# One layer of a Griffin decoder on one core: gates by Silu behind the chain's square root, and a written-out order for ScalarE and VectorE from the output projection's second group on

## The chip, the cores and the metric

The kernel runs on one core of a Trainium2 chip. The metric is the device time of one execution in microseconds. Of the kernel before, three runs were timed: median 1433.09 us (1432.62 to 1435.61).

## The reference

One token mixer of the kind "Griffin" and one gate from a per-layer embedding, for 1024 tokens of width 2048, in fp32 (names of the reference shortened):

```python
u = rms_norm(h, norm_pre) @ w_in              # 2048 -> 4096: gate half and x half
xc = causal_conv4(x_half) + conv_b
r, i = sigmoid(xc @ w_r + b_r), sigmoid(xc @ w_i + b_i)   # 8 blocks of 256
a = exp(-8 * softplus(lam) * r)
s = scan(s * a + sqrt(1 - a**2) * i * xc)     # along the tokens
y = (s * silu(gate)) @ w_out
h = h + rms_norm(y, norm_post)
out = h + sigmoid(h @ w_gate) * (p @ w_proj)  # the PLE block
```

## The kernel before

**Tiles and products.** Tokens lie along the free axis in two halves `h` of T = 512, channels on 128 partitions. The three large products (called x for `w_in`, y for `w_out`, h for `w_gate`) are taken by a Strassen-like scheme of seven products m1, m2, m7, m6, m3, m4, m5 of half the size. Each output tile `p` of each of the seven is a *unit*: 8 operand tiles times three matmuls of 128x128 by 128x512 (`mm3`, L116 to L118: high times high, high times low, low times high part), since every fp32 number is split in two parts of the matmul's type: `split` has ScalarE make the high part (L106) and VectorE the low one (L107). `m7` takes operands named t3, `m6` those named t2, `m4` t4, `m5` t1.

**The order of the work.** The program is a list of units. Each has stages some units ahead of its matmuls (`product`): LOAD (a DMA on SP's queue, 4 or 7 units ahead), ADD (the second block of the weight is accumulated onto it by a DMA that POOL issues, 5 ahead, L423), PART (the split, 3 ahead). `later` and `put` move stores to DRAM one or more units behind the tile that they store; POOL issues them too (L195). SP's and POOL's order is that of the program. ScalarE's, VectorE's and TensorE's is chosen by a scheduler. The main loop does this for each unit:

```python
            for f in late.pop(at, ()):
                f()
            for rank, j, f in sorted(begun.pop(at, ()), key=lambda b: b[:2]):
                f()
            s["mm"]()
```

**Stages.** The first half of the tokens goes through the x product, then the second; between the last products of x stand the block weights' matmuls (`ri`) and the chain steps. A *chain* step (h, n), n from 0 to 7, follows its `ri` unit for two channel tiles: on ScalarE two Sigmoids each for r and i (L310, L311), Tanh (L314), Exp (L318), three Squares (L319 to L321), Sqrt (L323); on VectorE the products and the scan in between and, for h = 1, the multiply by the gate (L335). It works in one buffer `rq`, so a chain step's first Sigmoid waits for the last multiply of the step before. The convolution of the next step and its split `x` (for the next `ri` unit) come behind the root. "Chain 1", "chain 3" below are the steps (1, 1) and (1, 3).

**Gates.** In `x_mm`, m4 of tile p gives gate g0_p of the first half, m5 that of the second (`gs`). Both are made by a Sigmoid into the PSUM bank (L582, L594) and a multiply on VectorE (L583, L595); g0_p is then multiplied by the recurrence's stored result (L584) and stored on POOL's queue.

**Behind the x product** come y's m1, m2, then in groups of four p the units m7, m6, m3, then m4; then the PLE block (`mm_ple`, four units of 48 matmuls, evacuations of tokens' half 0 on ScalarE, L694, of half 1 on VectorE, L696; each of the 32 tiles is stored); then y's m5; then h in the same manner, whose units end with `emit_out`. `norm_z1`, `norm_z2` make the post-norm's factors, `h_first` and `h_second` the sums of h, `fetch` reads stored operands back, `keep` splits them. Small tiles come from the pool `vecs` of seven buffers of 128x512; PSUM has eight banks.

## Time and profile before

| | |
|---|---|
| median of three runs | 1433.09 us |
| profiled execution | 1431.73 us, span 1430.0 us |
| mean granted TensorE clock | 0.986 |
| busy: TensorE, VectorE, ScalarE, GpSimd | 1384.3, 972.8, 719.3, 272.1 us |
| DMA | 358.81 MB, mean 251 GB/s |

Times in the profile count from the span's start. "Busy" counts instructions that do work; a wait is what an engine sat idle and the semaphore that ended it. A granted clock of 1.0 is 2.4 GHz, one of 0.5 is 1.2 GHz.

### The profile page before, as it was taken

Reading aid. Unit: us, or ns where it says so; the run is one execution under the profiler, and the core shown is the slowest. Engines: PE = TensorE matmul, PEld = TensorE weight load, DVE = VectorE, ACT = ScalarE, POOL = GpSimd, SP = SyncE. Lnnn points to the kernel's source line nnn. Section 1 sums busy time; section 2 is a strip of 40 time slices with the busy share of each in tenths; the row PEclk is TensorE's granted clock in tenths of the full one; section 3 lists DMA queues with packets and bytes.
Section 4 is the critical chain, followed back from the end, with each engine's and each line's share of the span. In section 5 each row is a group of like instructions: output and inputs, shape, how many; then the busy total and the mean of one; then the engine's idle time right before and its main releaser. Section 6 shows DMA issues by size and latency. Waiting matters only on the chain.

```text
span 1430.0 us, 17152 instructions
## 1 busy us (share of the span) xinstructions
PE 1384.3 (97%) x6025; PEld 1133.6 (79%) x6025; DVE 972.8 (68%) x1299; ACT 719.3 (50%) x936; POOL 272.1 (19%) x422
## 2 busy tenths in 40 slices
PE   9999999999999999989799999999999999999997
PEld 6888787878887888878677778888787887888886
DVE  8588768566665776777898954364479795538576
ACT  8332257475757543877888652332335334324332
POOL 0113331221211110111102421100242132211021
PEclk9999999999999999999999999999999999999999
DMA  9769899877767896576677999760899699989795
GB/s 356 249 229 311 279 304 249 251 166 215 186 178 179 273 313 203 157 216 206 191 261 262 340 334 263 175 205 35 290 354 365 219 357 351 268 214 290 235 331 177
DMA packets 125815, 358.81 MB, mean 251 GB/s; under 512 B 15904, under 2 KB 16288, under 8 KB 125728
## 3 DMA queue, kind: packets, MB, share of 16 engines
q1 hardware_dynamic: 83232, 210.88, 41.8%
q0 software_dynamic: 42496, 146.83, 39.6%
q8 instruction: 47, 0.77, 0.2%
q14 instruction: 40, 0.33, 0.1%
HBM read 277.95 MB, written 79.69 MB: 250 GB/s over the span
## 4 chain that ended last, share of the span: by engine, by line
PE 48%; issue 23%; DMA 11%; DVE 8%; ACT 5%; POOL 4%; SPq 0%; POOLq 0%; DVEq 0%; ACTq 0%
PE hm L118 5%; PE hm L117 5%; PE hm L116 5%; PE ym L116 5%; PE ym L118 5%; PE ym L117 5%; PE xm L118 3%; PE xm L117 3%; PE xm L116 3%; POOL sp L195 2%; DMA fxb<-sp 2%; POOL x_m L423 2%; DMA sp<-rq 1%; DVE xc L283 1%; PE pp L116 1%
## 5 line engine op out<-in xcount | busy, mean ns | idle before, releaser
L423 POOL DMA_DIRECT2D x_m<-in_w_in x64 | 57.8, 949 | 135.8 <-DVE wlo_x7m L107 17.8
L283 DVE SCALAR_TENSOR_TENSOR xc<-xbp,cst,xc 128x512 f32<-128x512 f32 x96 | 66.9, 746 | 0.4 <-ACT xc L280 0.3
L116 PE MATMUL ri<-x,whi_ri 128*128 128x512 f32 x128 | 50.0, 419 | 15.2 <-ACT x L106 15.2
L195 POOL DMA_DIRECT2D sp<-g x32 | 18.9, 633 | 210.6 <-DVE g L584 180.3
L117 PE MATMUL ri<-x,whi_ri 128*128 128x512 f32 x128 | 52.0, 407 | 0.5 <-DVE x L107 0.5
L118 PE MATMUL ri<-x,wlo_ri 128*128 128x512 f32 x128 | 51.4, 402 | 0.0
L717 POOL DMA_DIRECT2D out_t<-sg x32 | 17.5, 546 | 144.8 <-DVE sg L716 141.8
L423 POOL DMA_DIRECT2D h_m<-in_w_gate x32 | 28.7, 1031 | 83.0 <-DVE wlo_h4m L107 24.8
L116 PEld LDWEIGHTS ri<-x,whi_ri 128*128 128x128 f32 x128 | 25.0, 199 | 22.7 <-ACT x L106 17.1
L423 POOL DMA_DIRECT2D y_m<-in_w_out x32 | 29.1, 999 | 72.5 <-DVE wlo_y4m L107 26.9
L310 ACT ACT_TABLE_LOAD x12 | 15.4, 1283 | 38.6 <-DMA sp<-rq 21.3
L713 DVE TENSOR_TENSOR sg<-uh,hm 128x512 f32<-128x512 f32 x24 | 15.8, 685 | 25.3 <-PE hm L118 25.3
L280 ACT ACTIVATE xc<-xbp,cst 128x512 f32<-128x512 f32 x32 | 24.3, 805 | 14.8 <-DMA xbp<-sp 10.5
L106 ACT ACTIVATE x<-xc 128x1024 fp32r<-128x1024 f32 x16 | 16.8, 1053 | 28.8 <-DVE xc L283 28.8
L117 PEld LDWEIGHTS ri<-x,whi_ri 128*128 128x128 f32 x128 | 25.0, 196 | 7.6 <-DVE x L107 1.4
L195 POOL DMA_DIRECT2D sp<-ux x16 | 8.8, 551 | 113.4 <-DVE ux L577 104.8
L118 PEld LDWEIGHTS ri<-x,wlo_ri 128*128 128x128 f32 x128 | 24.9, 194 | 6.0
L310 ACT ACTIVATE rq<-ri,cst 128x512 f32<-128x512 f32 x32 | 21.2, 686 | 13.0 <-DVE g L335 6.9
L116 PE MATMUL pp<-p,whi_ple 128*128 128x512 f32 x64 | 25.7, 405 | 1.8 <-ACT p L106 1.8
L106 ACT ACTIVATE x_t<-xu 128x512 fp32r<-128x512 f32 x8 | 5.1, 634 | 44.0 <-DVE xu L349 43.9
L195 POOL DMA_DIRECT2D sp<-z x16 | 8.7, 546 | 91.4 <-DVE z L613 74.1
L107 DVE TENSOR_TENSOR x_t<-fxt,x_t 128x512 fp32r<-128x512 f32 x24 | 16.0, 690 | 14.6 <-ACT x_t L106 14.5
(722 smaller groups left out, 4956.7 us busy)
## 6 DMA issues: line engine op xcount, KB each, us to landing
x_m<-in_w_in SPq DMA_DIRECT2D x72, 512.0 KB, 5.6
x_m<-in_w_in POOLq DMA_DIRECT2D x64, 512.0 KB, 8.0
y_m<-in_w_out SPq DMA_DIRECT2D x40, 512.0 KB, 6.7
h_m<-in_w_gate SPq DMA_DIRECT2D x40, 512.0 KB, 8.8
y_m<-in_w_out POOLq DMA_DIRECT2D x32, 512.0 KB, 9.5
o<-sp SPq DMA_DIRECT2D x64, 256.0 KB, 6.6
h_m<-in_w_gate POOLq DMA_DIRECT2D x32, 512.0 KB, 9.2
raw_ri<-in_w_ri SPq DMA_DIRECT2D x16, 512.0 KB, 5.0
```

Of the source, the lines that this page charges most:

```text
L106: nc.scalar.activation(hi, src, AF.Copy)
L107: nc.vector.tensor_tensor(lo, src, hi.bitcast(F32), ALU.subtract)
L116: nc.tensor.matmul(ps, whi, ahi, start=start, stop=False, skip_group_check=more)
L117: nc.tensor.matmul(ps, whi, alo, start=False, stop=False, skip_group_check=more)
L118: nc.tensor.matmul(ps, wlo, ahi, start=False, stop=stop, skip_group_check=more)
L195: nc.gpsimd.dma_start(t, src)
L280: nc.scalar.activation(xc[:, s], xbp[:, s, 3 : T + 3], AF.Identity, bias=col(C_CB, ct), scale=col(C_CW + 48, ct))
L283: nc.vector.scalar_tensor_tensor(xc[:, s], xbp[:, s, j : j + T], col(C_CW + 16 * j, ct), xc[:, s], op0=ALU.mult, op1=ALU.add)
L310: nc.scalar.activation(R[:, s], banks[0][s], AF.Sigmoid, bias=col(C_BR, ct))
L423: nc.gpsimd.dma_start(u["raw"], w[(p, *ADDED[name])], accum_op=ALU.add)
L713: nc.vector.tensor_tensor(sg, part, b, ALU.subtract if h == 0 else ALU.add)
L717: later(1, lambda: nc.gpsimd.dma_start(out[h, :, dt, :], sg))
```

## The change

1. *Gates.* Sigmoid into PSUM and multiply become one Silu in place. From the second half's first `ri` unit on, gates are put in a list and issued on ScalarE behind the Sqrt of a chain step, two units after it in the program; those of m4 with p of 12 and more are issued at once.
2. *Main loop.* The stages PRE, LOAD and ADD now stand ahead of the late stores, PART behind them.
3. *By hand.* From the y product's second group on (`o2`, its first m7 unit) ScalarE and VectorE also follow the program. There PART comes behind the unit's evacuation; further evacuation work (`rest`) and splits of fetched operands (`next_turn`) behind that; fetched operands are used two units after their load is issued, not one.
4. *PLE.* The block moves behind y's m5, in eight units of 24 matmuls; all its evacuations are on ScalarE. The norm's factors are made in three steps; `h_first` begins in m5.

```diff
@@ main loop
             at = now[0]
+            todo = sorted(begun.pop(at, ()), key=lambda b: b[:2])
+            splits = [f for rank, j, f in todo if rank == PART]
+            for rank, j, f in todo:
+                if rank != PART:
+                    f()
             for f in late.pop(at, ()):
                 f()
-            for rank, j, f in sorted(begun.pop(at, ()), key=lambda b: b[:2]):
+            if not by_hand[0]:
+                for f in splits:
+                    f()
+            rest = s["mm"]()
+            if by_hand[0]:
+                for f in splits:
+                    f()
+            if rest:
+                rest()
+            now[0] += 1
+            for f in tail.pop(at, ()):
                 f()
-            s["mm"]()
-            now[0] += 1
@@ chain
-        nc.scalar.activation(Q, Q, AF.Sqrt)
+        root = nc.scalar.activation(Q, Q, AF.Sqrt)
+        if h == 1:
+            later(2, lambda: open_gates(root.ins))
@@ ahead of x_mm
+    def gate(f, at_once=False):
+        if waits_gates[0] and not at_once:
+            gates.append(f)
+        else:
+            f()
+
+    def open_gates(behind):
+        with tc.issue_after(behind):
+            for f in gates:
+                f()
+        gates.clear()
@@ x_mm, m4 and m5
-            nc.scalar.activation(b, g, AF.Sigmoid)
-            nc.vector.tensor_tensor(g, g, b, ALU.mult)
-            nc.vector.tensor_tensor(g, g, h0.pop(p), ALU.mult)
-            put((("b11", "b21")[s], n), yd, g)
+
+            def gated():
+                nc.scalar.activation(g, g, AF.Silu)
+                nc.vector.tensor_tensor(g, g, h0.pop(p), ALU.mult)
+                put((("b11", "b21")[s], n), yd, g)
+
+            gate(gated, p >= NK - 4)
...
-            nc.scalar.activation(b, g, AF.Sigmoid)
-            nc.vector.tensor_tensor(g, g, b, ALU.mult)
+            gate(lambda: nc.scalar.activation(g, g, AF.Silu))
@@ fetched operands (h_first, h_second and h_one likewise)
-            keep("h", name, n, t[:, 0])
+            next_turn(lambda: keep("h", name, n, t[:, 0]))
@@ mm_ple
-        for dd in range(4):
-            dt = 4 * i + dd
+        for dd in range(2):
+            dt = 2 * i + dd
...
-                if h == 0:
-                    nc.scalar.activation(t, b, AF.Copy)
-                else:
-                    nc.vector.tensor_copy(t, b)
+                nc.scalar.activation(t, b, AF.Copy)
@@ y product, PLE block
+    def begin_by_hand():
+
+        after.enter_context(tc.manual_schedule(engines={mybir.EngineType.Activation, mybir.EngineType.DVE}))
+        by_hand[0] = True
+
...
-    spread(o2 + 2, 0.75, fetches("y", yd, "b22"))
-    spread(o3 - 7, 1, fetches("y", yd, "t4"))
-    spread(o3, 1, fetches("y", yd, "t1"))
-    hook(len(orders) - 2, lambda: load_p(0))
-    hook(len(orders) - 1, lambda: load_p(1))
+    spread(o2 + 2, 0.75, fetches("y", yd, "b22"), 2)
+    spread(o3 - 7, 1, fetches("y", yd, "t4"), 2)
+    spread(o3, 1, fetches("y", yd, "t1"), 2)
+    hook(HAND, begin_by_hand)
     strassen("y", w_out, orders, emit_z, hooks, park=True, inserts=inserts_b)
...
-    for i in range(4):
-        plain(w_ple[i], f"ple{i}", lambda u, i=i: mm_ple(u, i))
...
+    for i in range(3):
+        hook(i, lambda i=i: norm_z(i, 0))
+    spread(1, 2, [lambda n=n: h_first(n) for n in range(3)], 2)
+    hook(4, lambda: load_p(0))
+    hook(5, lambda: load_p(1))
     strassen("y", w_out, [(p, "m5") for p in range(NB)], emit_z, hooks)
+    uses = {}
+    for i in range(KH):
+        plain(w_ple[i], f"ple{i}", lambda u, i=i: mm_ple(u, i), 512)
+        for f in uses.pop(i, ()):
+            do(f)
+        if i < 5:
+            got = []
+            do(lambda got=got, i=i: got.append(h_first(i + 3)))
+            uses.setdefault(i + 2, []).append(lambda got=got: got.pop()())
+        if i < 3:
+            do(lambda i=i: norm_z(i, 1))
```

**Where instructions move.** POOL, around the weight of x's m5, p = 12 (`x12_m5`), before:

```order
L195 DMA sp114_5145<-g0_11_5134 128x512
L423 DMA x11_m5_5050<-in_w_in 128x1024
L195 DMA sp115_5232<-g0_12_5221 128x512
L423 DMA x12_m5_5149<-in_w_in 128x1024
```

and in the change:

```order
L206 DMA sp113_5165<-g0_10_4962 128x512
L206 DMA sp114_5167<-g0_11_5108 128x512
L436 DMA x12_m5_5118<-in_w_in 128x1024
L206 DMA sp115_5211<-g0_12_5198 128x512
```

The accumulation onto `x12_m5` now stands ahead of the store of gate g0_12 and behind that of g0_11. (Numbers of spilled tiles `sp` count on and differ.)

ScalarE in chain 3, from its third Sigmoid to the split of `x12_m5`, before:

```order
L311 ACTIVATE rq1_3_5327<-ri1_3_10_5301,cst_80 128x512
L106 ACTIVATE whi_x14m4_5295<-x14_m4_5234 128x1024
L582 ACTIVATE xm4_12_5196<-g0_12_5221 128x512
L311 ACTIVATE rq1_3_5327<-ri1_3_11_5302,cst_80 128x512
L314 ACTIVATE rq1_3_5327<-rq1_3_5327,dk_90 128x512 x2
L318 ACT_TABLE_LOAD
L318 ACTIVATE rq1_3_5327<-rq1_3_5327,dk_90 128x512
L594 ACT_TABLE_LOAD
L594 ACTIVATE xm5_10_5241<-g5_5266 128x512
L318 ACT_TABLE_LOAD
L318 ACTIVATE rq1_3_5327<-rq1_3_5327,dk_90 128x512
L106 ACTIVATE whi_x12m5_5350<-x12_m5_5149 128x1024
```

and in the change, from the chain's start on (the split of `x12_m5` is the next row):

```order
L321 ACT_TABLE_LOAD
L321 ACTIVATE rq1_3_5301<-ri1_3_00_5273,cst_80 128x512
L321 ACTIVATE rq1_3_5301<-ri1_3_01_5274,cst_80 128x512
L612 ACT_TABLE_LOAD
L612 ACTIVATE g0_12_5198<-g0_12_5198 128x512
L106 ACTIVATE whi_x14m4_5269<-x14_m4_5208 128x1024
L322 ACT_TABLE_LOAD
L322 ACTIVATE rq1_3_5301<-ri1_3_10_5275,cst_80 128x512
L322 ACTIVATE rq1_3_5301<-ri1_3_11_5276,cst_80 128x512
L325 ACTIVATE rq1_3_5301<-rq1_3_5301,dk_90 128x512 x2
L329 ACT_TABLE_LOAD
L329 ACTIVATE rq1_3_5301<-rq1_3_5301,dk_90 128x512 x2
```

Gate `g5` (m5, p = 10) has left the place between the two Exps; gate g0_12 stands between the Sigmoids with a table load on each side, and the chain begins with a load.

ScalarE in the y product's m7 units, before:

```order
L106 ACTIVATE y_t22_6757<-fyt22_6714 128x512
L150 ACTIVATE sq_z0_60_6666<-z60_6664 128x512
L106 ACTIVATE y_t23_6760<-fyt22_6714 128x512
L106 ACTIVATE y_t24_6798<-fyt24_6763 128x512
L106 ACTIVATE y_t25_6801<-fyt24_6763 128x512
L106 ACTIVATE y_t26_6840<-fyt26_6804 128x512
L106 ACTIVATE y_t27_6843<-fyt26_6804 128x512
L106 ACTIVATE whi_y2m7_6678<-y2_m7_6479 128x1024
```

and in the change:

```order
L106 ACTIVATE y_t22_6725<-fyt22_6682 128x512
L153 ACTIVATE sq_z0_60_6634<-z60_6632 128x512
L106 ACTIVATE y_t23_6728<-fyt22_6682 128x512
L106 ACTIVATE whi_y2m7_6646<-y2_m7_6447 128x1024
L641 ACTIVATE z70_6674<-ym1_7_6510 128x512
L153 ACTIVATE sq_z0_70_6676<-z70_6674 128x512
L106 ACTIVATE whi_y3m7_6688<-y3_m7_6489 128x1024
L529 ACTIVATE uy0_6717<-ym7_0_6692 128x512
L529 ACTIVATE uy1_6762<-ym7_1_6737 128x512
L106 ACTIVATE whi_y0m6_6764<-y0_m7_6351 128x1024
L106 ACTIVATE y_t24_6768<-fyt24_6731 128x512
```

The splits of the weights for m7's third and fourth unit have moved ahead of the fetched operands y_t24 and those behind it, which m6 uses.

## Rows read from the trace of the kernel before

**Rows 1.** Page, part 1: busy us, share of the span, instructions, by engine.
```profile
PE 1384.3 (97%) x6025; PEld 1133.6 (79%) x6025; DVE 972.8 (68%) x1299; ACT 719.3 (50%) x936; POOL 272.1 (19%) x422
```

**Rows 2.** Waits of TensorE: engine, line, waited for, us in total, times, longest.
```profile
PE ri L116 <- ACT x L106: 15.2, 4, 7.6
PE ym L116 <- ACT whi_y2m L106: 3.5, 1, 3.5
PE ym L118 <- DVE wlo_y5m L107: 3.4, 2, 2.0
PE hm L116 <- ACT whi_h1m L106: 2.9, 1, 2.9
...
PE pp L116 <- ACT p L106: 1.8, 1, 1.8
```

**Rows 3.** Windows of core 0: length, busy us (instructions), clock, DMA share, GB/s.
```profile
678.80:705.80 27.00, 19.11 (x73) 14.88 (x73) 25.66 (x31) 20.83 (x27) 3.91 (x6) 0.87 0.55 154
616.80:640.30 23.50, 19.32 (x73) 15.32 (x72) 20.58 (x25) 16.01 (x21) 2.52 (x4) 0.85 0.62 188
839.00:857.00 18.00, 14.44 (x51) 10.93 (x50) 12.32 (x17) 11.88 (x20) 4.08 (x5) 0.81 1.06 352
1198.00:1215.00 17.00, 13.57 (x52) 10.42 (x51) 12.12 (x17) 11.07 (x17) 2.91 (x4) 0.90 1.04 355
```

**Rows 4.** Timeline of TensorE: start, us, engine, line, form, [idle before <-releaser].
```profile
626.55 0.79 PE L116 MATMUL ri<-x,whi_ri 128*128 128x512 f32 x1 [4.18 <-ACT x L106]
...
683.72 0.39 PE L117 MATMUL xm<-x_t,whi_x12m 128*128 128x512 f32 x1
...
684.63 0.39 PE L118 MATMUL xm<-x_t,wlo_x12m 128*128 128x512 f32 x1
692.63 0.79 PE L116 MATMUL ri<-x,whi_ri 128*128 128x512 f32 x1 [7.62 <-ACT x L106]
```

**Rows 5.** Timeline of ScalarE, chain 1, in front of the squares.
```profile
612.95 1.06 ACT L106 ACTIVATE whi_x8m<-x_m 128x1024 fp32r<-128x1024 f32 x1 [2.16 <-DMA x_m<-in_w_in]
```

**Rows 6.** Timeline of ScalarE, chain 3.
```profile
668.93 1.28 ACT L594 ACT_TABLE_LOAD   x1
...
670.85 1.28 ACT L318 ACT_TABLE_LOAD   x1
...
677.36 1.06 ACT L106 ACTIVATE whi_x12m<-x_m 128x1024 fp32r<-128x1024 f32 x1 [4.49 <-DMA x_m<-in_w_in]
```

**Rows 7.** Timeline of POOL there, and the landing of the accumulation (us, last).
```profile
667.82 0.56 POOL L195 DMA_DIRECT2D sp<-g  x1 [18.68 <-DVE g L584]
668.37 0.95 POOL L423 DMA_DIRECT2D x_m<-in_w_in  x1
...
x_m<-in_w_in POOLq DMA_DIRECT2D x1, 512.0 KB, 8.9
```

**Rows 8.** Timeline of ScalarE, y product's m7; landing of the weight's accumulation issued at 825.24.
```profile
845.48 0.63 ACT L106 ACTIVATE y_t<-fyt 128x512 fp32r<-128x512 f32 x1 [2.50 <-DMA fyt<-sp]
...
847.07 1.04 ACT L106 ACTIVATE whi_y2m<-y_m 128x1024 fp32r<-128x1024 f32 x1
...
y_m<-in_w_out POOLq DMA_DIRECT2D x1, 512.0 KB, 13.8
```

**Rows 9.** Timeline of ScalarE, h product's m7.
```profile
1198.37 0.63 ACT L106 ACTIVATE h_t<-fht 128x512 fp32r<-128x512 f32 x1 [7.33 <-DMA fht<-sp]
```

**Rows 10.** Groups by line: busy us, mean ns, idle before; ScalarE, then VectorE.
```profile
L582 ACT ACTIVATE xm<-g 128x512 f32<-128x512 f32 x16 | 9.5, 593 | 0.1
...
L583 DVE TENSOR_TENSOR g<-g,xm 128x512 f32<-128x512 f32 x16 | 10.9, 681 | 6.4 <-ACT xm L582 6.4
```

**Rows 11.** PLE block: a window, VectorE's wait for stores, landing of the stores.
```profile
1020.00:1035.00 15.00, 15.00 (x69) 12.44 (x68) 5.40 (x12) 4.25 (x7) 5.84 (x10) 0.95 1.04 368
...
DVE pp L696 <- DMA sp<-pp: 10.4, 4, 3.6
...
sp<-pp POOLq DMA_DIRECT2D x26, 256.0 KB, 7.0
```

More of the change, by code (lines that the diff above doesn't have):

```diff
@@ L127, in rstd_a, with rstd_n @@
         nc.scalar.activation(s, v, AF.Sqrt)
+        return v, s, r, t
+    def rstd_n(v, s, r, t):
         nc.vector.reciprocal(r, s)
@@ L155, in trunk_kernel @@
     st = {}
+    after = ExitStack()
     def unit(mm, stages):
@@ L180, in plain, with next_turn @@
         return u
-    late = {}
-    now, n_spills = [0], [0]
+    late, tail = {}, {}
+    now, n_spills, by_hand = [0], [0], [False]
+    def next_turn(f):
+        if by_hand[0]:
+            tail.setdefault(now[0], []).append(f)
+        else:
+            f()
     def later(k, f):
@@ L511, in mm @@
             elif name == "m2":
-                emit(p, 0, 0, b, None)
+                return emit(p, 0, 0, b, None)
             elif name == "m7":
@@ L522, in mm @@
             elif name == "m4":
-                emit(p, 1, 0, b, t[:, 1])
+                return emit(p, 1, 0, b, t[:, 1])
             elif name == "m5":
-                emit(p, 1, 1, b, t[:, 1])
-                emit(p, 0, 1, b, t[:, 0])
+                rests = emit(p, 1, 1, b, t[:, 1]), emit(p, 0, 1, b, t[:, 0])
+                return lambda: [f() for f in rests]
         products(key, w, orders, mm, pre, hooks, inserts)
+    gates, waits_gates = [], [False]
+    def gate(f, at_once=False):
+        if waits_gates[0] and not at_once:
+            gates.append(f)
+        else:
+            f()
[4 more added lines that the diff above has]
+        gates.clear()
     m1d, ud, xbank, h0 = {}, {}, {}, {}
@@ L616, in emit_z @@
         st["nz", h] = seen + 1
-        square(z, seen == 0, h, f"z{h}_{p}{i}")
+        return lambda: square(z, seen == 0, h, f"z{h}_{p}{i}")
     hd = {}
@@ L637, in use @@
             make_h(0, n, z, x)
-            keep("h", "b11", n, z[:, 0])
-            keep("h", "b21", n, z[:, 1])
+            next_turn(lambda: [keep("h", name, n, z[:, i]) for i, name in enumerate(("b11", "b21"))])
         return use
@@ L655, in use @@
             put(("t2", n), hold, x[:, 1])
-            keep("h", "t3", n, x[:, 0])
+            next_turn(lambda: keep("h", "t3", n, x[:, 0]))
         return use
@@ L713, in emit_out, with rest @@
             nc.vector.tensor_tensor(sg, part, b, ALU.subtract if h == 0 else ALU.add)
-            nc.scalar.activation(sg, sg, AF.Sigmoid, scale=-1.0 if (i, h) == (0, 1) else 1.0)
-        nc.vector.tensor_tensor(sg, sg, o[:, 0], ALU.mult)
-        nc.vector.tensor_tensor(sg, sg, o[:, 1], ALU.add)
-        later(1, lambda: nc.gpsimd.dma_start(out[h, :, dt, :], sg))
+        def rest():
+            if part is not None:
+                nc.scalar.activation(sg, sg, AF.Sigmoid, scale=-1.0 if (i, h) == (0, 1) else 1.0)
+            nc.vector.tensor_tensor(sg, sg, o[:, 0], ALU.mult)
+            nc.vector.tensor_tensor(sg, sg, o[:, 1], ALU.add)
+            later(1, lambda: nc.gpsimd.dma_start(out[h, :, dt, :], sg))
+        return rest
     def norm_x(h):
-        st["r1"] = rstd_a(st["acc", h], f"x{h}")
+        st["r1"] = rstd_n(*rstd_a(st["acc", h], f"x{h}"))
     def norm_x2(h):
@@ L729, in hook, with spread @@
         hooks.setdefault(at, []).append(f)
-    def spread(at, every, fs):
+    def spread(at, every, fs, lag=1):
         for i, f in enumerate(fs):
@@ L820, in trunk_kernel @@
             at(o + 6, lambda h=h, n=n: block_ri(h, n), True)
+            if h == 1 and n == 0:
+                at(o + 6, lambda n=n: waits_gates.__setitem__(0, True))
     at(o + 6, lambda: do(lambda: pools["swap"]()), True)
@@ L825, in trunk_kernel, with norm_z @@
     hooks = hooks_b
-    def norm_z1(h):
-        st["rz"] = rstd_a(st["acc", h], f"z{h}")
-    def norm_z2(h):
-        st["rstd2", h] = rstd_b(st["rz"], h, f"z{h}")
+    def norm_z(step, h):
+        if step == 0:
+            st["rz"] = rstd_a(st["acc", h], f"z{h}")
+        elif step == 1:
+            st["rz"] = rstd_n(*st["rz"])
+        else:
+            st["rstd2", h] = rstd_b(st["rz"], h, f"z{h}")
     orders, o2, o3 = grouped(range(NB), range(NB), [(p, "m4") for p in range(NB)])
+    HAND = o2
@@ L872, in trunk_kernel @@
+    spread(o2 - 1, 0.75, fetches("h", hold, "t2"), 2)
+    spread(o2 + 2, 0.75, [lambda n=n: fetch("h", {("b22", k): hd[1, 2 * k + 1] for k in (n, n + 1)}, "b22", n) for n in range(0, KH, 2)], 2)
+    spread(o3 - 8, 0.5, [lambda n=n: h_one("t4", n) for n in range(KH)], 2)
+    spread(o3 - 4, 0.5, [lambda n=n: h_one("t1", n) for n in range(KH)], 2)
     strassen("h", w_gate, orders, emit_out, hooks, early_out, True)
@@ L879, in trunk_kernel @@
             begun.setdefault(max(0, j - ahead), []).append((rank, j, f))
-    with ExitStack() as after:
+    with after:
         def opened(name):
```

29 lines of the change are left out of this document (6 added, 23 removed).

## The prediction

> **What bounds the kernel now.** The page's busy line comes first: TensorE is busy 1384.3 of 1430.0 us, and no other engine comes near [rows 1]. So the kernel is bound by TensorE, and a change that adds and removes no matmul can only give back what TensorE loses: the time it waits and the time it runs at the low clock after a wait. The list of TensorE's waits says for whom [rows 2]: 15.2 us in four waits of the block weights' matmuls (`ri`) for the chain step's split on ScalarE, 3.5 us for the high half of a weight of the y product, 3.4 us in two waits for a low half, 2.9 us for a high half of the h product, 1.8 us for the split of `p`.
>
> The windows give the price of a wait with what follows it. From one start to the next a matmul takes (684.63 - 683.72) / 4 = 0.2275 us [rows 4]; a stretch's length less its matmuls at that step is what it loses (a few records may be missing, so each figure is rough). 616.80 to 640.30: 23.5 - 73 x 0.2275 = 6.9 us. 678.80 to 705.80: 10.4 us. 839 to 857: 6.4 us. 1198 to 1215: 5.2 us [rows 3]. The second holds the longest wait, 7.62 us [rows 4], and its mean granted clock is 0.87, not 1.0: for a part of it the engine ran at the lower of its two levels (1.2 instead of 2.4 GHz), and that is the rest of the loss. A wait that goes takes this second part with it.
>
> Then the timelines say why ScalarE is late. In chain 1 its queue stood 2.16 us on a weight's DMA [rows 5]. In chain 3 it stood 4.49 us on the DMA of weight x12_m5, in front of the chain's squares; it also loaded a table for a gate, ran the gate and loaded the exponential's table again [rows 6]. The DMA was late because POOL, which issues in order, had waited 18.68 us on VectorE for the store of gate g0_12; the weight's accumulation came right behind, at 668.37, and took 8.9 us to land: 677.27, and ScalarE went on at 677.36 [rows 7].
>
> **The change part by part.** *Gates.* 32 Sigmoids and 32 multiplies become 32 Silus. The multiply takes 0.68 us [rows 10]: 32 x 0.68 = 22 us of VectorE. That engine isn't the bound, so I count it as nothing by itself; it shortens VectorE's part of the chain. A Silu is on no row; I take the Sigmoid's 0.59 us [rows 10]. A Silu needs its own table: by the order of instructions 65 loads stand where 61 stood, each 1.28 us [rows 6], so ScalarE pays 5.1 us more, but most of these loads move behind the square root, off the chain's path.
>
> The Trainium skill bears on this (ScalarE: Activation LUTs, "Table sets: the hidden batching unit" and "What ACT_TABLE_LOAD costs"): calls should be batched by set, and a switch costs about 2.66 us, a drain being added to the load. Here the trace disagrees on the price: between the end of one load (668.93 + 1.28 = 670.21) and the start of the next (670.85) lie 0.64 us, in which one gate of 0.59 us ran [rows 6, 10]. By that page four more loads would be 10.6 us of ScalarE, by the rows 5.1.
>
> *Chain 1.* The x split of the next block comes earlier by the wait of 2.16 us (its accumulation now stands ahead of the stores), by a load and gate between the exponential and the squares (1.28 + 0.59), and by three gates of 0.59 us that move behind the root; a load of the Sigmoid's table at the chain's start is added (1.28). Net 2.16 + 1.87 + 1.77 - 1.28 = 4.5 us, against a wait of 4.18 there [rows 4]. I count 6 of the 6.9 us as won.
>
> *Chain 3.* The wait of 4.49 us goes: the accumulation of x12_m5 now only follows g0_11's store, whose Silu stands behind the root of chain 2, so I count on an issue at least 4.5 us before the old 668.37. Load, gate and reload of the m5 gate (1.28 + 0.59 + 1.28) and one more gate (0.59) move behind the root. In return gate g0_12, which is not held back, now needs a load and a load back inside the sigmoids (2.57), and the chain's start a load (1.28). Net 4.49 + 3.74 - 3.85 = 4.4 of the 7.62 us; about 3.2 us of wait stay, with a stretch at the low clock behind it. I count 5 of 10.4 us as won. The other two waits (15.2 - 7.6 - 4.2 = 3.4 us [rows 2, 4]) come after a chain that starts 4 us or more earlier; with their part of low clock I put them at 6 us, and count 3. Chain stage: -14 us; bounds -4 (the reordered tables eat it) and -22 (all of it).
>
> *Hand order in y.* ScalarE split `whi_y2m7` behind four operands that it had to wait for, the last but one with an idle of 2.50 us; it came at 847.07 [rows 8], and TensorE had wanted it 3.5 us before that [rows 2]. Those operands belong to m6, whose units begin only behind m7's four. The weight's accumulation was issued at 825.24 and took 13.8 us: 839.0, so 5 us before TensorE's need. In the new order the split stands ahead of these operands. -6 of 6.4 us; bounds -1 (the weights come later as the whole stretch moves forward and the DMA share there is 1.06 [rows 3]) and -6.4.
>
> *Hand order in h.* The same: ScalarE idled 7.33 us for the first operand of m6 [rows 9] with the splits of m7 behind it. -4.5 of 5.2 us; bounds 0 and -5.2.
>
> *PLE block moved behind y's m5.* `p` is now loaded and split two units ahead, so the 1.8 us wait goes, with its low clock some 3: -3, bounds 0 and -3.4. Of the two waits for `wlo_y5m` the one in m5 should go by the hand order: -1.5, bounds 0 and -2. All 32 evacuations of the block are now ScalarE's, 0.6 us each against 1.36 us (6 x 0.2275) that TensorE takes for one: 19 us of 44, hidden by TensorE as long as a free tile is there. If not, TensorE waits when the 8 PSUM banks are full. Before, TensorE ran 15.00 of 15 us in this block although evacuations waited 10.4 us for stores [rows 11], so the banks covered it. In the new place the pool of seven tiles also holds two of the norm's, and about 19.4 MB must move in 43.5 us (32 stores of 0.26 MB, five h loads of 1.05 and their stores, and weights), 446 GB/s, while the row has 368 [rows 11], by which it would take 53 us: +9. Nearest is the old block, which carried the same 32 stores and no less beside them with no wait, because loads may trail. I take +3, bounds 0 and +11.
>
> By the Trainium skill (Perfetto Trace Analysis, "Roofline") one core's 16 DMA engines give about 435 GB/s together; the wide row stays below that at 368. By that figure the 19.4 MB take 44.6 us, and the term would be +1.
>
> *Rest.* Start, first half of x and the tail are left as they were; SP's queue gets four more loads; 0, bounds -3 and +4.
>
> **Sum.** -14 - 6 - 4.5 - 3 - 1.5 + 3 = -26 from the profiled execution's 1431.73 us: 1405.7. The median of the runs is 1.36 us above that execution, so the forecast for the median is 1407.
>
> **Rivals.** *A: the chain stays the bound.* VectorE's last multiply of one chain frees the buffer for the next chain's sigmoids, and now a table load follows that wait each time. If the loads weigh on the path in every chain, the stage gives only 4 us and the rest 12: about 1431.7 - 16 + 1.4 = 1417. For it: the added loads at each start; against it: the waits on DMA were not the chain's own work. The batching rule of the Trainium skill, told above, speaks for this rival.
>
> *B: slower, by the stores of the PLE block.* Five free tiles, each held for evacuation, issue and landing: 0.6 (as a gate [rows 10]) + 0.6 (as the store's issue [rows 7]) + 7.0 [rows 11] = 8.2 us, give 32 tiles in 52 us against 43.5, and the eight banks, 1.36 us each, cover up to 11 us, so nothing is lost. If a store takes the 13.8 us that a transfer of the same queue took under load [rows 8], a tile is held 15 us and 32 need 96 us: 96 - 43.5 - 11 = +41.5, against gains of 29, so 1433.1 + 12.5 = 1446. It decides from a landing of about 12 us on, where the stores cost some 32 us. Against it: the row of this block says 7.0, and TensorE was busy throughout.
>
> *C: no change.* The weights of m7 come too late for the splits wherever these stand, because the DMA is full there (share 1.06 [rows 3]), and chain 3's wait is only handed from one DMA to the next: 1431 to 1434. Against it: the landings at 839.0 and 677.27 with their causes.
>
> **How the numbers follow.** The forecast with sums from -15 to -38 gets 0.61, A 0.17, B 0.15, C 0.07. A measurement of this kernel tells about 0.2%, 2.9 us, from no change. Faster: the forecast and A, less 0.02 for A's tail: 0.76. Same: C and a bit of A and B where the price about equals what the rest wins: 0.09. Slower: 0.15. Low end: chain stage -22, the rest -18, no price for the stores: 1393, rounded to 1394. High end: A with the stores at +11: 1428; it leaves out B and C, together 22 in 100.
>
> **What would show it.** Right: in the list of waits `ri <- ACT x` falls from 15.2 to 3 to 6 us with one wait of 2 to 4 us at chain 3; ScalarE's idle in front of `whi_x12m` is gone; the waits for `whi_y2m`, `whi_h1m` and `p` are gone; VectorE's busy time falls by some 30 us; 64 to 66 table loads. Wrong: waits of `pp` or of the first h matmuls on stores or on `zr` loads; `ri` waits that stay above 10 us; new waits for weight splits in m5, where VectorE's queue now holds the norm and h's first sums.

## The result, and the profile after

The changed kernel took **1421.05 us** (median; 1417.82 to 1423.12), the kernel before 1432.86 in the same comparison: ratio 0.9917, 95% interval 0.9897 to 0.9936. That is a gain of 11.8 us where 26 were forecast: right in sign, inside the range, and less than half of the size. The profiled execution took 1417.82 us, 13.9 less than the profiled one before; the accounts below go by these two. It is the shortest of the changed kernel's four executions, 3.2 us under their median, so a single row is good to a few microseconds.

Page, part 1, of the kernel after ([rows 1] before):

```profile
PE 1380.6 (97%) x6025; PEld 1128.1 (80%) x6025; DVE 947.1 (67%) x1255; ACT 729.5 (52%) x960; POOL 271.8 (19%) x422
```

TensorE is the bound as before. VectorE lost 25.7 us, ScalarE gained 10.2, and neither of the two is the bound. TensorE's waits after (engine, line, waited for, us in total, times, longest), against [rows 2]:

```profile
PE ri L116 <- ACT x L106: 3.7, 3, 2.9
PE hm L116 <- ACT h_b L106: 3.2, 1, 3.2
PE xm L118 <- DVE wlo_x4m L107: 2.3, 1, 2.3
PE rb_z L141 <- ACT pp L722: 2.2, 1, 2.2
...
PE hm L117 <- DVE h_t L107: 1.4, 1, 1.4
...
PE ym L118 <- DVE wlo_y5m L107: 0.8, 1, 0.8
```

The `ri` waits for ScalarE fell from 15.2 to 3.7 us; those for `whi_y2m`, `whi_h1m` and `p` are gone. But `h_b`, `rb_z` (the norm's factors), `wlo_x4m` and `h_t` are new. Cut at the starts of certain matmuls in TensorE's two timelines, the 13.9 us come out like this:

| stretch | before | after | change | forecast |
|---|---|---|---|---|
| start to the second half's first `ri` unit | 566.7 | 572.9 | +6.3 | 0 |
| from there to the last `ri` unit (chain stage) | 216.1 | 201.4 | -14.7 | -14 |
| to the end of y's m4 | 231.7 | 225.4 | -6.3 | -6 |
| y's m5 and PLE block | 94.9 | 93.5 | -1.4 | -1.5 |
| first h unit to h's m7 | 88.9 | 94.5 | +5.6 | 0 |
| h's m7 to m4 | 136.2 | 130.6 | -5.6 | -4.5 |
| h's m4 to TensorE's end | 87.2 | 89.6 | +2.4 | 0 |
| tail | | | -0.2 | 0 |

(About 1.9 us of the norm's small matmuls and what is slow behind them moved from the first h row into the PLE block; without them the PLE row is -3.3 and that h row +7.5.) The four rows with a forecast came within 1.1 us of it. The missing 12 us stand in three rows to which the forecast gave nothing.

**Chain 3, as forecast.** ScalarE's timeline after (start, us, engine, line, form, [idle before <-releaser]), to set beside [rows 6]:

```profile
660.65 1.27 ACT L321 ACTIVATE rq<-ri,cst 128x512 f32<-128x512 f32 x2
661.94 1.28 ACT L612 ACT_TABLE_LOAD   x1
663.23 0.63 ACT L612 ACTIVATE g<-g 128x512 f32<-128x512 f32 x1
...
664.83 1.28 ACT L322 ACT_TABLE_LOAD   x1
...
671.17 1.04 ACT L106 ACTIVATE whi_x12m<-x_m 128x1024 fp32r<-128x1024 f32 x1
```

The split of `x12_m5` has no idle in front of it. POOL issued that weight's accumulation at 660.85, 7.5 us earlier than in [rows 7], and the block weights' matmuls wait 2.95 us where they waited 7.62 [rows 4]:

```profile
660.85 0.91 POOL L436 DMA_DIRECT2D x_m<-in_w_in  x1 [0.16 <-issue]
```

```profile
686.28 2.07 PE L116 MATMUL ri<-x,whi_ri 128*128 128x512 f32 x4 [2.95 <-ACT x L106]
```

The same rows settle the price of a load: it ends at 661.94 + 1.28 = 663.22 and the Silu starts at 663.23. The Trainium skill (ScalarE: Activation LUTs, "What ACT_TABLE_LOAD costs") adds a drain to each switch; the trace shows none here, as before.

**y's m7, as forecast.** ScalarE's timeline after; in [rows 8] the split of `y2_m7` came behind the fetched operands:

```profile
833.93 1.05 ACT L106 ACTIVATE whi_y2m<-y_m 128x1024 fp32r<-128x1024 f32 x1
...
836.02 1.04 ACT L106 ACTIVATE whi_y3m<-y_m 128x1024 fp32r<-128x1024 f32 x1
...
838.88 1.15 ACT L106 ACTIVATE y_t<-fyt 128x512 fp32r<-128x512 f32 x2
```

**The first half, not forecast.** POOL's and ScalarE's timelines after, around the second chain step of the tokens' first half:

```profile
275.49 0.87 POOL L436 DMA_DIRECT2D x_m<-in_w_in  x1 [1.76 <-DVE wlo_x5m L107]
276.04 1.47 POOL L206 DMA_DIRECT2D sp<-rq  x2
```

```profile
287.53 1.28 ACT L321 ACT_TABLE_LOAD   x1 [10.31 <-DMA sp<-rq]
```

Before, at the same step:

```profile
271.35 0.56 POOL L195 DMA_DIRECT2D sp<-ux  x1 [9.51 <-DVE ux L577]
...
272.51 1.46 POOL L195 DMA_DIRECT2D sp<-rq  x2
```

```profile
284.15 1.28 ACT L310 ACT_TABLE_LOAD   x1 [7.70 <-DMA sp<-rq]
```

In the first half a chain step's result is stored from the buffer `rq`, and the next step's first Sigmoid waits until the store has landed, not only for VectorE's last operation. (The last multiply, named above for all steps, is what frees the buffer in the second half.) The new loop puts a unit's accumulation ahead of its stores, so these two stores now stand on POOL behind one accumulation more. Here it is the one that unit m6 of p = 5 makes onto the buffer `x5_m7`, and it waits until VectorE has split what m7 needs from there. The stores go out 3.5 us later, and ScalarE stands 10.31 us in front of a chain instead of 7.70, with weight splits queued behind it. Over the first half (150 to 600 us; first the kernel before, then after):

```profile
ACT L310 <- DMA sp<-rq: 21.3, 4, 7.7
```

```profile
ACT L321 <- DMA sp<-rq: 35.0, 7, 10.3
```

**The start of h, not forecast.** POOL's timeline after, where the PLE block now stands:

```profile
1053.51 1.07 POOL L206 DMA_DIRECT2D sp<-zr  x2 [10.31 <-DVE zr L656]
1054.58 3.20 POOL L206 DMA_DIRECT2D sp<-pp  x6
```

ScalarE's waits between 1043 and 1100 us, and the DMA share in two windows of the block (length, busy us by engine, clock, share, GB/s):

```profile
ACT pp L722 <- DMA sp<-pp: 13.1, 8, 3.4
...
ACT pp L722 <- PE pp L118: 5.0, 1, 5.0
...
ACT h_b L106 <- DVE zr L656: 1.4, 1, 1.4
```

```profile
1060.00:1075.00 15.00, 12.77 (x61) 10.44 (x60) 6.84 (x14) 8.64 (x16) 6.45 (x12) 1.00 0.99 377
1075.00:1093.00 18.00, 18.00 (x81) 14.89 (x81) 11.81 (x16) 9.50 (x17) 6.42 (x12) 1.00 0.97 374
```

Stores of finished PLE tiles (`pp`) stand on POOL behind stores of h's first sums (`zr`), which wait up to 10.31 us for VectorE; then six go at once. Until they land the pool has no free tile, and ScalarE, in program order now, stands in front of its next evacuation with the splits of h's first operands behind it. (The wait of 5.0 us stands under TensorE in the list, but TensorE had written that bank at about 1056. The wait ends at 1061.46, and the first of the six stores, issued at 1054.58, landed at 1061.35: it is a wait for a store too.) TensorE meets both ends of this:

```profile
1064.99 1.13 PE L141 MATMUL rb_z<-ident,n_z 128*128 128x128 f32 x8 [2.23 <-ACT pp L722]
1101.32 0.50 PE L116 MATMUL hm<-h_b,whi_h0m 128*128 128x512 f32 x1 [3.22 <-ACT h_b L106]
1102.67 0.79 PE L117 MATMUL hm<-h_b,whi_h0m 128*128 128x512 f32 x1 [0.84 <-DVE h_b L107]
1103.26 0.63 PE L118 MATMUL hm<-h_b,wlo_h0m 128*128 128x512 f32 x1
```

A matmul shows 0.63 us behind the wait against 0.39 elsewhere [rows 4], and the window from 1095 to 1110 us has a mean granted clock of 0.77: for a part of it the engine ran at 1.2 instead of 2.4 GHz.

```profile
1095.00:1110.00 15.00, 10.94 (x35) 8.21 (x34) 8.02 (x10) 5.98 (x10) 5.90 (x12) 0.77 0.87 302
```

**The last stage, not forecast.** The first matmuls of h's last m5 group wait for an operand that is now split two units after its load:

```profile
1339.31 0.50 PE L116 MATMUL hm<-h_t,whi_h0m 128*128 128x512 f32 x1 [0.48 <-ACT h_t L106]
1341.19 0.50 PE L117 MATMUL hm<-h_t,whi_h0m 128*128 128x512 f32 x1 [1.38 <-DVE h_t L107]
```

### The profile page after: what moved, and what is told of

Same layout as the page of the kernel before. It is cut to its first block, busy times and chain, and to the rows that moved or that the text cites. A ratio compares the mean times of both kernels' runs of the same rounds, so it can differ in the third digit from the quotient of the medians.

```text
span 1416.0 us, 17194 instructions
## 1 busy us (share of the span) xinstructions
PE 1380.6 (97%) x6025; PEld 1128.1 (80%) x6025; DVE 947.1 (67%) x1255; ACT 729.5 (52%) x960; POOL 271.8 (19%) x422
## 5 line engine op out<-in xcount | busy, mean ns | idle before, releaser
L106 ACT ACTIVATE x<-xc 128x1024 fp32r<-128x1024 f32 x16 | 16.8, 1053 | 32.6 <-DVE xc L294 32.6
L722 ACT ACTIVATE pp<-pp 128x512 f32<-128x512 f32 x32 | 18.1, 596 | 20.7 <-DMA sp<-pp 13.1
L206 POOL DMA_DIRECT2D sp<-ux x16 | 9.7, 605 | 89.8 <-DVE ux L605 89.6
L106 ACT ACTIVATE x_t<-fxt 128x512 fp32r<-128x512 f32 x24 | 14.2, 622 | 23.2 <-DMA fxt<-sp 23.2
L116 PE MATMUL pp<-p,whi_ple 128*128 128x512 f32 x64 | 25.1, 392 | 0.0
L117 PE MATMUL pp<-p,whi_ple 128*128 128x512 f32 x64 | 24.9, 389 | 0.0
```

The costliest lines, as they stand in the source:

```text
L106: nc.scalar.activation(hi, src, AF.Copy)
L116: nc.tensor.matmul(ps, whi, ahi, start=start, stop=False, skip_group_check=more)
L117: nc.tensor.matmul(ps, whi, alo, start=False, stop=False, skip_group_check=more)
L206: nc.gpsimd.dma_start(t, src)
L722: nc.scalar.activation(t, b, AF.Copy)
```

## The experiments

Times are medians with the ratio to the kernel before and its 95% interval. "First half" is the start of the second half's first `ri` unit, "chain stage" as in the table; these two and the waits are from one profiled execution of each kernel.

**1. Where the loop's order costs and where it pays.** Edits of the kernel after: the old order (late stores first) up to the second half's first `ri` unit (e1), or up to the order by hand (e2).

```diff
-            for rank, j, f in todo:
+            old = not (waits_gates[0] or by_hand[0])   # e1; e2: not by_hand[0]
+            stores = late.pop(at, ())
+            if old:
+                for f in stores:
+                    f()
+                stores = ()
+            for rank, j, f in todo:
                 if rank != PART:
                     f()
-            for f in late.pop(at, ()):
+            for f in stores:
                 f()
```

> The changed kernel with the old main loop (stores ahead of PRE, LOAD and ADD) up to the second half's first ri unit. Theory: the new loop order costs the first half 5 to 6 us, because a weight's accumulation that waits for its buffer now holds up the stores behind it on POOL. Then that ri unit starts at 567 to 568 us instead of 572.9, the chain stage behind it is as in the changed kernel (201 us from the first to the last ri unit), and the median is 1414 to 1417. Rival: the 6 us are chance of the DMA's timing; then the ri unit starts at 572 to 574 and the median stays at 1421.

> The changed kernel with the old main loop up to the hand order's start, so in the whole x product. Theory: the new loop order costs the first half some 6 us and gives the chain stage 3 us (the accumulation of x12_m5). Then the second half's first ri unit starts at 563 to 570 us, ScalarE waits for x12_m5 again, TensorE's longest ri wait is 5 to 7 us, the chain stage takes 203 to 206 us (201 in the changed kernel), and the median is 1411 to 1415, 2 to 4 above the kernel with the old loop in the first half only (1409.6). Rival: with the gates behind the root the accumulation is early enough anyway; then the chain stage takes 201 to 202 us and the median is 1408 to 1411.

Edits of the kernel before: the new loop alone (e3), the new gates alone (e4).

```diff
# e3
+            todo = sorted(begun.pop(at, ()), key=lambda b: b[:2])
+            for rank, j, f in todo:
+                if rank != PART:
+                    f()
             for f in late.pop(at, ()):
                 f()
-            for rank, j, f in sorted(begun.pop(at, ()), key=lambda b: b[:2]):
-                f()
+            for rank, j, f in todo:
+                if rank == PART:
+                    f()
# e4: open_gates, gate, gated and the Silus of the change
+        root = nc.scalar.activation(Q, Q, AF.Sqrt)
+        if h == 1:
+            later(2, lambda: open_gates(root.ins))
...
+            gate(gated, p >= NK - 4)
...
+            gate(lambda: nc.scalar.activation(g, g, AF.Silu))
```

> The kernel before with the new main loop alone (PRE, LOAD, ADD ahead of the stores, PART behind). Theory: the accumulation of x12_m5 is early, ScalarE's wait of 4.49 us for it goes, TensorE's waits for ri fall from 15.2 to 8 to 11 us, and the first half loses 5 to 6 us: median 1429 to 1434, no clear change. Rival (the chain stage's gain comes from the gates alone): ri waits stay at 14 to 16 us and the median rises to 1437 to 1440.

> The kernel before with the gates alone (Silu in place, held until behind a chain's square root; p of 12 and more at once). Theory: the first half is as before (second half's first ri unit at 566 to 568 us), the wait of ScalarE for x12_m5 stays (3 to 6 us) as its accumulation stands behind the store of g0_12; ri waits fall from 15.2 to 7 to 11 us; median 1424 to 1429. Rival (the gates bring the whole gain of the chain stage): ri waits under 5 us and the median at 1416 to 1420. Other rival (the tables eat what the order gives): ri waits of 14 us or more, median 1431 to 1436.

| | us | ratio | first half | chain stage | ScalarE's wait for `sp<-rq` |
|---|---|---|---|---|---|
| before | 1432.86 | | 566.7 | 216.1 | 21.3 |
| after | 1421.05 | 0.9917 (0.9897 to 0.9936) | 572.9 | 201.4 | 35.0 |
| e1 | 1409.56 | 0.9844 (0.982 to 0.9868) | 569.8 | 201.4 | 19.9 |
| e2 | 1412.76 | 0.9861 (0.9844 to 0.9879) | 562.8 | 204.7 | 20.2 |
| e3 | 1435.5 | 1.0021 (1.0 to 1.0042) | 574.3 | 206.8 | 35.8 |
| e4 | 1419.77 | 0.9907 (0.9887 to 0.9928) | 563.1 | 204.2 | 21.6 |

The new loop costs in the first half and pays in the chain stage. Alone it wins 9.3 us there (e3) and loses 7.6 ahead of it: nothing in sum by the profiles, and 1.0021 with 1.0 at the edge of the interval by the medians. The gates alone win 11.9 in the chain stage (e4), both together 14.7; the two parts cure much of the same wait. What the loop adds to the gates is the wait on the weight's DMA: with the old loop ScalarE still stands for `x12_m5` (e4, between 500 and 800 us 3.3 us in that wait) and `ri` waits 6.4 us once. TensorE's list in e4:

```profile
PE ri L116 <- ACT x L106: 7.1, 3, 6.4
```

e2 came as expected, e3 1.5 us above. e1 and e4 came out some 4 us below what was expected, e4 inside its first rival's range; that rival's sign, `ri` waits under 5 us, did not come (7.1). e1's profile is its longest execution, 5 us above its median.

One profile of each is a weak basis for the first half, but there are 13 whose kernels differ ahead of that `ri` unit only in the loop and in the form of the first gates. With the old loop (before, e1, e2, e4 and e9 to e11 below) it takes 562.8 to 569.8 us, 566.5 in the mean, and ScalarE's wait for `sp<-rq` is 19.9 to 21.9 us. With the new one (after, e3 and e5 to e8 below) it takes 572.9 to 578.3 us, 575.1 in the mean, with a wait of 32.6 to 37.2 us. The ranges do not touch, and the means are 8.5 us apart, more than the 6.3 of the table.

**2. Which store?** Two stores of the first half move behind accumulations: `ux` (parts of the products, put two units late) and `rq`. Kernel after, with the one (e12) or the other (e13) a unit earlier.

```diff
-            put(p, ud, us.pop(("x", p)), 2)
+            put(p, ud, us.pop(("x", p)), 1)       # e12
-            put(2 * n + s, hs, Q[:, s], 6)
+            put(2 * n + s, hs, Q[:, s], 5)        # e13
```

> The changed kernel with the stores of the first half's sums (ux) issued one unit earlier, so that they stand ahead of the same accumulations as with the old loop. Theory: an accumulation that waits for its buffer holds the ux stores behind it on POOL; so ux's buffers come free late, SP's weight loads wait for them, and the fetched operands behind those on SP come late. With the stores earlier, ScalarE's wait for fetched operands (23.2 us) falls to 18 or 19 as with the old loop, the second half's first ri unit starts at 563 to 571 us instead of 573 to 578, and the median is 1411 to 1416. Rival: other stores (rq, xt) or the stores' own wait for VectorE matter; then the ri unit starts at 572 us or later and the median stays at 1419 to 1423.

> The changed kernel with the stores of the first half's recurrence (rq) issued one unit earlier, so that they stand ahead of the same accumulation as with the old loop. Theory: with the new loop they stand behind one accumulation more, which waits for a buffer; the next chain waits for their landing, since rq is one buffer, and the weight splits behind the chain on ScalarE come late. With the stores earlier ScalarE's wait for sp<-rq falls from 35 us to 19 to 22 us, the second half's first ri unit starts at 563 to 570 us, and the median is 1409 to 1414. Rival: the wait for rq is a companion, and the late fetched operands (23 us) set the loss; then the ri unit starts at 571 us or later and the median stays at 1418 to 1423.

e12 missed: 1432.81 us, 0.9999 (0.9984 to 1.0013), first half 589.7; ScalarE's wait for `sp<-rq` rose to 48.0 us. The theory that `ux` was the cause fell. e13: **1405.86 us, 0.9823 (0.9787 to 0.986)**, first half 562.0, that wait 3.4 us where 19 to 22 were expected:

```profile
ACT L321 <- DMA sp<-rq: 3.4, 2, 2.3
```

TensorE's waits between 200 and 590 us, the kernel after and then e13:

```profile
PE xm L118 <- DVE wlo_x4m L107: 2.3, 1, 2.3
PE xm L118 <- DVE wlo_x6m L107: 1.6, 1, 1.6
PE xm L116 <- ACT whi_x2m L106: 1.2, 1, 1.2
PE xm L118 <- DVE wlo_x15m L107: 1.1, 1, 1.1
PE xm L118 <- DVE wlo_x2m L107: 0.8, 1, 0.8
PE xm L118 <- DVE wlo_x7m L107: 0.5, 1, 0.5
```

```profile
PE xm L118 <- DVE wlo_x3m L107: 0.4, 1, 0.4
```

One unit for one kind of store takes 7.5 us of waits down to 0.4; before there were 3.7. So the change made a wait longer that the kernel before had in part too. e13 does more than give the stores their old place back. POOL's timeline in e13, at the same step as above:

```profile
267.90 0.89 POOL L436 DMA_DIRECT2D x_m<-in_w_in  x1 [8.15 <-DVE wlo_x4m L107]
268.45 1.48 POOL L206 DMA_DIRECT2D sp<-rq  x2
```

They stand between the same two accumulations as before the change, but a store of `ux` that stood ahead of them there, at 271.35 after 9.51 us of waiting for VectorE, now comes behind them. So e13 shows that these stores are the cause, but what it wins, 15.2 us in the medians, is not only the price of the new order; e1, which restores the old one, wins 11.5, and the two are not told apart.

**3. Is it the place behind the root?** Kernel before with Silu for Sigmoid and multiply, each issued at once and not held (73 table loads, 65 in e4):

```diff
# e4, but
-        if waits_gates[0] and not at_once:
+        if False:
```

> The kernel before with Silu gates that are not held: each is issued where the scheduler puts it (73 table loads, 65 with the gates held, 61 before). Theory: the position behind the root brings the gates' gain; at once, each chain pays Silu's table and the load back, the waits for ri stay at 12 us or more and the chain stage takes 212 to 222 us (216 before, 204 with the gates held): median 1429 to 1440. Rival: VectorE's 32 multiplies less bring it, wherever the Silu stands; then the chain stage takes 204 to 208 us and the median is 1419 to 1424.

1438.7 us, 1.0038 (1.0021 to 1.0056), so slower than before; chain stage 221.6. TensorE's list:

```profile
PE ri L116 <- ACT x L106: 18.7, 6, 4.8
```

VectorE was 19 us less busy (953.7) and the time rose: whatever the multiplies were worth, the added table loads cost more. e4 has the same operations, and its chain stage takes 204.2 us, so the gain of the gates is their place, with the loads that it saves. Holding two more gates (p = 12 and 13) as well:

```diff
-            gate(gated, p >= NK - 4)
+            gate(gated, p >= NK - 2)
```

> The changed kernel with the gates g0_12 and g0_13 held behind chain 3's root too (at once from p = 14 on). Theory: TensorE's last long ri wait (2.9 us before chain 4) comes from the loads of two tables inside chain 3; without them it falls under 0.5 us, and with its low clock 4 to 6 us go: median 1415 to 1418. Rival: the buffer's loop sets it, since VectorE's last multiply of chain 2 lets chain 3 start when it does; then 1.5 to 3 us of wait stay and the median is 1418 to 1422. Other rival: the y product's first operands, which are made of these gates, come later, and TensorE waits for y_b at its start.

1418.84 us, 0.9899 (0.9882 to 0.9916), chain stage 200.3 against 201.4: not told apart from the kernel after, and above the 1415 to 1418 that the theory gave. The 2.95 us of chain 3 are gone, and a wait of the same matmuls for a low half stands in their place:

```profile
PE ri L118 <- DVE wlo_ri L107: 2.5, 1, 2.5
```

**4. The PLE block.** The order of POOL's queue (e5: stores of `zr` one unit later) or too few tiles (e8: two more slots for PLE tiles)?

```diff
# e5
-    def make_h(h, p, z, x):
+    def make_h(h, p, z, x, k=1):
...
-            put((h, 2 * p + s), hd, z[:, s])
+            put((h, 2 * p + s), hd, z[:, s], k)
...
-            make_h(0, n, z, x)
+            make_h(0, n, z, x, 2)
# e8
+                j = 2 * dt + h
+                if j == 0:
+                    st["ppx"] = act("ppx", F32)
+                if j % 7 in (2, 5):
+                    t = st["ppx"][:, (j % 7) // 5]
+                else:
+                    t = one(f"pp{h}_{dt}")
-                t = one(f"pp{h}_{dt}")
```

> The changed kernel with the stores of h's first half (zr) issued one unit later, behind the stores of the PLE block's tiles of the unit before. Theory: POOL's in-order wait for VectorE's zr keeps the PLE tiles from being stored; without it ScalarE's evacuations keep up, TensorE's waits at rb_z (2.2 us) and at the h product's first unit (h_b, 3.2 + 0.8 us, with the low clock 7.6 in all) go, and the median falls by 6 to 9 us to 1412 to 1415. Rival: the DMA is full there (share 0.97 to 0.99 in the block) and the stores land no earlier wherever they are issued; then both waits stay within 1 us and the median stays at 1419 to 1423.

> The changed kernel with two more tiles for the PLE block's results (two halves of a free operand tile take every second and fifth of seven). Theory: five tiles, each held some 7 us from evacuation to landing, are too few for one every 1.36 us; with seven ScalarE's waits for sp<-pp fall from 13.1 to under 5 us, the waits at rb_z and at the h product's first unit go, and the stretch from the block's start to h's m7 gets 6 to 9 us shorter: median 1412 to 1415. Rival (POOL's order alone): the stores are still behind zr's and the waits stay above 8 us; median 1418 to 1422.

e5 1416.98 us, 0.9894 (0.9876 to 0.9912); e8 1417.58, 0.9892 (0.9877 to 0.9906). Both missed the 1412 to 1415 us that were expected. By the whole time neither is told apart from the kernel after; by the stretch they are meant for they are: from the last `ri` unit to h's m7 the kernel before took 415.6 us, after 413.4, e5 408.2, e8 408.0. Nine other profiles with this block as in the kernel after or as before lie between 413.0 and 417.2. The wait of `rb_z` is gone in both, and the wait for `h_b` falls to 1.6 in e5, to 2.7 in e8:

```profile
PE hm L116 <- ACT h_b L106: 1.6, 1, 1.6
```

So each theory had about half. With both (e10 below) it is 403.6, and no `h_b` wait is left. ScalarE's waits for the stores show why one repair is not enough. In the kernel after they are 13.1 us and the 5.0 named above; in e5, with the order alone, 13.3; in e8, with the tiles alone, 11.0, where under 5 were expected; in e10 1.8. The rows of e5, then of e10 between 1030 and 1110 us:

```profile
ACT pp L722 <- DMA sp<-pp: 13.3, 10, 2.3
```

```profile
ACT pp L728 <- DMA sp<-pp: 1.8, 1, 1.8
```

With e5 the waits are shorter and more (2.3 us at the longest, not 5.0).

**5. The last stage.** The operands t4 and t1 of h begin a unit earlier:

```diff
-    spread(o3 - 8, 0.5, [lambda n=n: h_one("t4", n) for n in range(KH)], 2)
+    spread(o3 - 9, 0.5, [lambda n=n: h_one("t4", n) for n in range(KH)], 2)
-    spread(o3 - 4, 0.5, [lambda n=n: h_one("t1", n) for n in range(KH)], 2)
+    spread(o3 - 5, 0.5, [lambda n=n: h_one("t1", n) for n in range(KH)], 2)
```

> The changed kernel with h's operands t4 and t1 (h_one) begun one unit earlier. Theory: used two units after their load instead of one, the last t1 operand is split 2 us too late for m5's first unit; begun earlier the waits for h_t (0.5 + 1.4 us) go and the last stage (m4, m5) takes 87 us instead of 89.6: median 1418 to 1419.5. Rival: VectorE is busy with the units' outputs there and the split comes late wherever its load begins; then 1 us or more of these waits stays.

1413.89 us, 0.9867 (0.9843 to 0.9891). The waits for `h_t` are gone and the stage takes 87.2 us, as before the change. The median is 7.2 us below the kernel after, and 4 below what was expected; the stage gives 2.4 of that, the two profiled executions differ by 3.1, and e6's four executions spread over 7.6 us. Where the rest comes from is not shown.

**6. All repairs.** e10: e1, e5, e8 and e6 together. e11: with the gates of e7 as well. e14: e11, but the new loop throughout and the `rq` stores of e13 in place of e1.

> The changed kernel with the old loop in the first half, zr's stores one unit later, two more tiles for the PLE block's results and t4, t1 begun one unit earlier. Theory: the four repairs act in four stages and add: second half's first ri unit at 563 to 570 us, chain stage 201, last ri unit to h's first unit 315, from there to m7 87 to 90, last stage 87: median 1399 to 1404. Rival: zr's stores and the tiles cure one and the same wait, and the DMA gets full; then h's first units still wait 3 us or more and the median is 1405 to 1409.

> The same with the gates g0_12 and g0_13 held as well. Theory: chain 3's wait goes from 2.9 us to one of 2.5 for the low half of the next block weight, as in the changed kernel with this edit: 0 to 2 us below the kernel with the other four repairs. Rival: y's first operands come late and it is slower.

> The changed kernel with rq's stores one unit earlier (the new loop kept throughout), zr's stores one unit later, two more tiles for the PLE block's results, t4 and t1 begun one unit earlier, g0_12 and g0_13 held. Theory: the first half is then as in the run with the rq stores alone (ri unit at 562 to 565 us), everything behind it as in the run with all repairs, some 829 us from there to the span's end: median 1392 to 1397, 3 to 7 us below the version with the old loop in the first half (1399.5). Rival: the first half's 562 us were a lucky execution; then the median is 1398 to 1401.

e10 1399.52 us, 0.9767 (0.9743 to 0.979). e11 1399.47, 0.9761 (0.9738 to 0.9785): the held gates add nothing that can be told. e14 **1396.44 us, 0.9749 (0.9727 to 0.9772)**, the fastest median, below both kernels; its interval overlaps those of e10 and e11. All three medians came as expected. TensorE's two longest waits in e14:

```profile
PE xm L118 <- DVE wlo_x15m L107: 5.1, 1, 5.1
PE ri L118 <- DVE wlo_ri L107: 2.5, 1, 2.5
```

The wait for `wlo_x15m` lies in the first 200 us. It is 0.8 us there in the profile of the kernel after and 2.2 in e13, which is the same code up to there; what sets it stays open. It goes with the difference between the first halves of e13 (562.0) and e14 (565.4). Between e1 (569.8) and e2 (562.8), whose `rq` waits are the same, another wait differs: `wlo_x3m`, 3.9 us in e1 and 0.3 in e2.

## Why the prediction was right in sign and wrong in size

- **Chain stage**, -14 forecast, -14.7 measured. Right, with its signs: `ri` waits of 3.7 us in all (3 to 6 were named), one of 2.9 at chain 3 (2 to 4), the idle in front of `whi_x12m` gone, 65 table loads in the trace (64 to 66). VectorE's busy time fell by 25.7 us where some 30 were named. The working added up what the gates and the loop win; e3 (-9.3) and e4 (-11.9) show that the two overlap.
- **Hand order**, y -6 and h -4.5: -6.3 and -5.6. Right in size, and the waits named are gone; e3, e4 and e9, which have neither the order by hand nor the later use of fetched operands, keep them (`whi_y2m` 3.8 to 5.0 us). No run takes the order by hand out by itself.
- **PLE**, p, `wlo_y5m` and stores together -1.5: -1.4 within the block. The price lies behind it: the start of h lost 5.6 us to the block's waits. This is where the term "+3 for the stores" was mis-sized. I gave it 0 to +11, and with the start of h it is about +3 + 5.6 = +8.6; e10, with both repairs, wins 9.8 us there. My working asked how long a store takes to land and counted five free tiles; it did not ask in which order POOL issues them. And it let the eight banks cover ScalarE's wait, which they do for the block's own matmuls, but not for the splits of h's operands that stand behind the evacuations on ScalarE.
- **Rest**, 0 (-3 to +4): **the step that failed.** "Start, first half of x and the tail are left as they were" was wrong: the loop runs from the first unit on, and the stores that move behind accumulations include the ones that the next chain step waits for. They cost 6.3 us in the two profiles and 8.5 in the means of 13; e13, which moves these stores alone, is 15.2 us below the kernel after by the medians. The last stage's 2.4 us fell under the same 0: that `h_one`'s operands are used two units after their load was in the diff, and I gave it no price. Together 8.7 us, where the bounds were -3 and +4.
- **The range** held, but not by the forecast's own sums: they ran from -15 to -38, and the gain, 13.9 us in the profiles and 11.8 in the medians, is smaller than any of them. The high end of 1428 came from rival A, and there the store term is counted twice: A's 12 us hold the +3 already, so with +11 it is 1425. Rival A's 1417 is nearer to the measured 1421 than the forecast's 1407, by chance: it gave the chain stage 4 us, and the stage won 14.7.
- **VectorE's multiplies**, counted as nothing by themselves: not settled. In e9 VectorE is 19 us less busy and the kernel is slower, but it has twelve more table loads than the kernel before; no run takes the multiplies away alone.
- **Rival A**, loads on the chain's path in every step: not in this kernel, but the mechanism is real, and e9 is it. With the gates behind the root the chain stage is shorter although the kernel has four loads more than before. The batching rule that spoke for A (Trainium skill, ScalarE: Activation LUTs, "Table sets: the hidden batching unit") says to do the calls of one table set together. By it the held gates are the better of the two, and e4 and e9 agree: 65 loads and 204.2 us against 73 and 221.6. The number of loads alone does not set the stage: the kernel before has 61 and takes 216.1.
- **Rival B**, tiles held by stores: the sign named for it, waits of the first h matmuls, came. Its price and condition did not: stores landed in 6.5 us at the median between 1050 and 1105 us, well under the 12 us from which I let it decide (by the working's own terms 12 us cost 30, not 32), and TensorE lost some 10 us, not 41. The tiles were held because the stores were issued late and because five of them are too few (e5, e8, e10).

```profile
sp<-pp POOLq DMA_DIRECT2D x32, 256.0 KB, 6.5
```

- By the Trainium skill (Perfetto Trace Analysis, "Roofline") 435 GB/s would be the limit in this block. The two windows above moved 377 and 374 GB/s at a share of 0.99 and 0.97, so the share was full below that figure; e5, e8 and e10 show that order and tiles set the loss all the same.
- **Rival C**, the weights too late wherever the splits stand: refuted by the y row, the h row and the split of `x12_m5`, which waits for no DMA.

## What to carry to other kernels

When a change turns the order of a loop that issues for an in-order queue, follow every kind of DMA in it over the whole run, not only where the change is meant to act: a store that frees a single buffer is part of the next step's path, and behind a load that itself waits for a buffer it inherits that wait. Replacing an operation by one with another table pays by where it is put; in the old place it was slower here. And when a block is moved, look at the queue that its stores join and at what stands first in it, before counting bandwidth.

## What the runs showed that I had not expected

One unit's shift of 16 stores (`rq`, two per chain step) moves the kernel by 15.2 us in the medians (11.1 in the profiles), about as much as the whole change did; the same shift of the `ux` stores made it 11.8 us slower. The first half got longer with ScalarE's wait for the `rq` stores from some 20 us on (566.5 us at 20, 575.1 at 35, 589.7 at 48 in e12) and hardly shorter below it (562.0 and 565.4 at 3). A Silu of 128x512 in place takes 0.62 us where the Sigmoid into PSUM took 0.59 [rows 10]. ScalarE's line of the m5 gates after (duration ns min/median/max):

```profile
L625 ACT ACTIVATE g<-g x16: 612/624/634, 531.1 to 745.8; 128x512 f32<-128x512 f32 x16
```
